# An RWKV layer whose k, r and v products run as plain fp32 on raw weights, with unpadded 64-row products and another order around the inversion

## Chip, cores and metric

The kernel runs on one core of a Trainium2 chip. What is compared is the device time of one execution in microseconds, the median of several. The profiled execution is one more, with a trace of every engine.

## What is computed

The program is a stack of layers on 256 tokens of width 1024: an RWKV time mix, a convolutional feed-forward, two attention layers and several gated feed-forward layers. Only the RWKV time mix is touched by the change:

```python
    xx = jnp.pad(x, ((0, 0), (1, 0), (0, 0)))[:, :-1] - x
    xr, xw, xk, xv, xa, xg = [x + xx * mu[i] for i in range(6)]
    r = xr @ w_rkv[0]
    k = xk @ w_rkv[1]
    v = xv @ w_rkv[2]
    w = -jax.nn.softplus(-(w_decay0 + jnp.tanh(xw @ w_decay1) @ w_decay2)) - 0.5
    a = jax.nn.sigmoid(a0 + (xa @ a1) @ a2)
    g = jax.nn.sigmoid(xg @ g1) @ g2
...
    def step(S, inp):
        r_t, d_t, k_t, v_t, a_t, b_t = inp
        sa = jnp.einsum('bhij,bhj->bhi', S, a_t)
        S = (S * d_t[:, :, None, :] + sa[..., None] * b_t[:, :, None, :]
             + v_t[..., None] * k_t[:, :, None, :])
        return S, jnp.einsum('bhij,bhj->bhi', S, r_t)
```

After the scan come a group norm per head, a bonus term, the gate g and the projection w_o.

## The kernel before

x is kept transposed (feature on the partition) as hT; xx is its difference to the token before. A mix is x + xx*mu for one 128-row chunk: VectorE makes the even chunks (L450), ScalarE and POOL the odd ones (L447, L448).

Weights come in units of 1 MB, on the queue of SyncE, into two raw slots: units 0 to 3 are k, 4 to 7 r, 8 to 11 v, 12 to 15 w_o. Each is split into a rounded part hi (L120, ScalarE, for units 0 and 1 also VectorE) and the rest lo (L122, VectorE; a table of bits in that line gives some quarters to POOL: one of units 0 and 1, all four of units 10 to 13). The activations are split as well (L138, L139), and mm3 (L146 to L148) forms one product from three matmuls of the fast fp32r type:

```python
        W['mm'].append(PE.matmul(o, lhsT=lh, rhs=rh, start=start, stop=False))
        PE.matmul(o, lhsT=lh, rhs=rl, start=False, stop=False)
        PE.matmul(o, lhsT=ll, rhs=rh, start=False, stop=stop)
```

The order is this. The LoRA products pw and pa (L474, L480) need eight mixes each, then pz (L498) in plain fp32 gives decay and a; a scan over time on VectorE (L508) makes the decay sums. k is four units (pk), with a norm per head behind each (pn, pnb); r is four units (pr), with the bonus products pq and pb. AR and KB hold the decayed r and a, and the decayed k and b, head pairs on 128 partitions.

The scan works on four chunks of 64 tokens. For each, M = KB' AR per head is a 64-row product. The kernel copies KB into a tile KZ whose other half is zero (L601) and so uses 128 rows; VectorE masks the result (L606). The diagonal 32x32 blocks of M are transposed into one batch of 32 triangular matrices (L616) and inverted together on VectorE, 31 steps of one product and one sum each (L623, L624), with n(j+1) elements per partition, n = 31 - j:

```python
                    V.tensor_tensor(out=tv, in0=XI[:, j + 1:32, j:j + 1].to_broadcast([P, n, j + 1]), in1=TL[:, j:j + 1, 0:j + 1].to_broadcast([P, n, j + 1]), op=ALU.mult)
                    V.tensor_tensor(out=TL[:, j + 1:32, 0:j + 1], in0=TL[:, j + 1:32, 0:j + 1], in1=tv, op=ALU.add)
```

Two transposes of the result (TtD at L626, TnD at L627) end this chain. Beside it TensorE forms v (pv), transposes KB (pkt), the gate's two products pg (L660, 128 columns) and pg2 (L661, 32 columns), and pgt (L674, L675). Behind the chain pgm and pwm (L693, L709) complete the inverse to 64x64 in Tt, with copies gm; means and centre subtract the head mean from v into vc and UV. Each chunk then takes pak (L745), ry (from chunk 1 on), their sum RHs, pu (L765, the inverse times RHs), psn (the new state) and py (the output). POOL forms the gate terms in five instructions for each half of 128 tokens (`gates`, L809 to L813) and issues broadcast loads of rows (L169); `gn` is the group norm on VectorE.

Each engine's instructions stand in one list; `tc.high_priority()` and `tc.issue_after` shift their place in it. Each engine works its list off in order.

## Time and profile before

| | us |
|---|---|
| median of 3 runs | 1377.85 (1376.36 to 1378.54) |
| profiled execution | 1378.07 |
| its span in the trace | 1376.4 |
| TensorE busy | 1321.2 (96%) |
| VectorE busy | 1071.2 (78%) |
| ScalarE busy | 840.4 (61%) |
| POOL busy | 129.3 (9%) |

The span is from the first to the last instruction of the trace; 1.67 us of the profiled execution lie outside it. A busy time is the sum over all instructions of an engine, so an engine can be far from full over the span and full in one stage. Matmuls are pipelined: the distance between their starts, not their duration, is what one costs.

### The profile page before, as it was taken

How to read it: one execution, taken by the hardware profiler on the slowest of the kernel's cores; microseconds unless marked ns; L12 is line 12 of the kernel's file. 1: busy time of each engine (PE TensorE's matmuls, PEld its weight loads, DVE VectorE, ACT ScalarE, POOL GpSimd, SP SyncE). 2: the span in 40 equal slices, each digit the busy share in tenths (PEclk: the TensorE clock that was granted, in tenths of full speed). 3: DMA queues.
4: the chain of work that ended last, by engine and by line, in shares of the span. 5: the costliest groups of instructions: out<-in, count | busy, mean ns of one | idle time of the engine just before them, and what ended most of it. 6: DMA issues, size and time to landing. Idle time of an engine off the chain costs nothing.

```text
span 1376.4 us, 21002 instructions
## 1 busy us (share of the span) xinstructions
PE 1321.2 (96%) x7776; PEld 1125.3 (82%) x7776; DVE 1071.2 (78%) x2296; ACT 840.4 (61%) x1793; POOL 129.3 (9%) x140
## 2 busy tenths in 40 slices
PE   6789888899999999999999999999999999999998
PEld 4788486688888977888888998888887788888887
DVE  8999968799888776998887986766668787576663
ACT  6675444677667874876667854655545766464551
POOL 3366380000000020000001000000000000000000
PEclk9999888999999999999999999999999999999999
DMA  5343202466553523565536554455553644265550
GB/s 212 125 152 111 74 2 92 154 233 226 185 193 128 184 92 107 199 235 202 202 131 225 200 193 158 172 212 191 199 189 118 254 155 151 78 229 192 197 192 31
DMA packets 35111, 226.30 MB, mean 164 GB/s; under 512 B 3744, under 2 KB 6208, under 8 KB 8896
## 3 DMA queue, kind: packets, MB, share of 16 engines
...
q8 instruction: 61, 1.00, 0.3%
...
## 4 chain that ended last, share of the span: by engine, by line
PE 83%; DVE 12%; ACT 3%; issue 1%; DMA 1%; POOL 1%; DVEq 0%; ACTq 0%; SPq 0%
PE pu L299 9%; PE pm L299 7%; PE pu L297 6%; PE md L148 4%; PE md L146 4%; PE md L147 4%; PE pm L297 4%; PE fd L146 3%; PE fd L147 3%; PE fd L148 3%; DVE lo L122 1%; DVE TL L624 1%; DVE tm L623 1%; PE pu L295 1%; PE gu L148 1%
## 5 line engine op out<-in xcount | busy, mean ns | idle before, releaser
L122 DVE TENSOR_TENSOR lo<-raw,hi 128x512 fp32r<-128x512 f32 x680 | 441.6, 692 | 79.0 <-ACT hi L120 76.9
L120 ACT CAST hi<-raw 128x512 fp32r<-128x512 f32 x696 | 387.5, 618 | 142.8 <-PE md L148 52.3
L299 PE MATMUL pu<-X_n_x,hi 128*128 128x512 f32 x560 | 142.1, 393 | 0.0
L299 PEld LDWEIGHTS pu<-X_n_x,hi 128*128 128x128 f32 x560 | 100.1, 189 | 17.5
L299 PE MATMUL pm<-X_ml_x,hi 128*128 128x512 f32 x392 | 99.7, 393 | 0.0
L297 PEld LDWEIGHTS pu<-X_n_x,lo 128*128 128x128 f32 x640 | 87.4, 190 | 6.2
L297 PE MATMUL pu<-X_n_x,lo 128*128 128x256 f32 x640 | 89.7, 283 | 0.0
L299 PEld LDWEIGHTS pm<-X_ml_x,hi 128*128 128x128 f32 x392 | 70.0, 189 | 12.2
L117 DVE SCALAR_TENSOR_TENSOR lo<-raw,cv,hi 128x256 fp32r<-128x256 f32 (+1 forms) x136 | 67.3, 560 | 14.1 <-ACT hi L116 14.1
L116 ACT ACTIVATE hi<-raw,cv 128x256 fp32r<-128x256 f32 (+1 forms) x136 | 65.9, 560 | 14.5 <-DMA raw<-in_wst 8.9
L305 DVE TENSOR_TENSOR r<-pm,r 128x256 f32<-128x256 f32 x56 | 23.6, 424 | 57.3 <-ACT r L304 57.3
L304 ACT COPY r<-pm 128x256 f32<-128x256 f32 x56 | 20.8, 372 | 74.3 <-PE pm L299 74.3
L297 PEld LDWEIGHTS pm<-X_ml_x,lo 128*128 128x128 f32 x448 | 61.2, 190 | 4.3
L297 PE MATMUL pm<-X_ml_x,lo 128*128 128x256 f32 x448 | 62.7, 282 | 0.0
L939 ACT ACTIVATE ab<-zs,cv 128x256 f32<-128x256 f32 x80 | 47.5, 600 | 16.8 <-DVE zs L305 16.7
L147 PE MATMUL md<-lo,md0h 128*128 128x512 f32 x128 | 49.9, 390 | 0.0
L146 PE MATMUL md<-hi,md0h 128*128 128x512 f32 x128 | 49.8, 389 | 0.0
L148 PE MATMUL md<-hi,md0l 128*128 128x512 f32 x128 | 49.8, 389 | 0.0
L146 PE MATMUL md<-hi,md1h 128*128 128x512 f32 x128 | 49.8, 389 | 0.0
L147 PE MATMUL md<-lo,md1h 128*128 128x512 f32 x128 | 49.8, 389 | 0.0
L148 PE MATMUL md<-hi,md1l 128*128 128x512 f32 x128 | 49.8, 389 | 0.0
L940 DVE SCALAR_TENSOR_TENSOR ab<-zs,cv,ab 128x255 f32<-128x255 f32 x80 | 38.3, 481 | 10.7 <-ACT ab L939 9.2
...
## 6 DMA issues: line engine op xcount, KB each, us to landing
...
```

What stands on the lines that cost most here:

```text
L116: A.activation(hi[:, q:q + w], r[:, q:q + w], AF.Copy, scale=g[:, j:j + 1])
L117: V.scalar_tensor_tensor(out=lo[:, q:q + w], in0=r[:, q:q + w], scalar=g[:, j:j + 1], in1=hi[:, q:q + w].bitcast(F32), op0=ALU.mult, op1=A ...
L120: (A.copy, V.tensor_copy, G.tensor_copy)[(40 if i < W['vhi'] else 0) // (1, 3, 9, 27)[q // SPL] % 3](hi[:, q:q + SPL], r[:, q:q + SPL])
L122: pe_.tensor_tensor(out=lo[:, q:q + SPL], in0=r[:, q:q + SPL], in1=hi[:, q:q + SPL].bitcast(F32), op=ALU.subtract)
L146: W['mm'].append(PE.matmul(o, lhsT=lh, rhs=rh, start=start, stop=False))
L147: PE.matmul(o, lhsT=lh, rhs=rl, start=False, stop=False)
L148: PE.matmul(o, lhsT=ll, rhs=rh, start=False, stop=stop)
L297: W['mm'].append(PE.matmul(pt[:, 0:T], lhsT=l3[:, k, fs], rhs=X2[:, 0, k, :], start=False, stop=False))
L299: PE.matmul(pt, lhsT=h3[:, k, fs], rhs=X2[:, :, k, :], start=False, stop=k == KD - 1)
L305: V.tensor_tensor(out=out, in0=pt[:, 0:T], in1=out, op=ALU.add)
L939: A.activation(ab[:, s, :], z, AF.Identity, bias=cw(3, fi), scale=cw(2, fi))
L940: V.scalar_tensor_tensor(out=ab[:, s, 1:T], in0=z[:, 0:T - 1], scalar=cw(1, fi), in1=ab[:, s, 1:T], op0=ALU.mult, op1=ALU.add)
```

## The change

- The units 0 to 11 stay raw, in six rotating slots (kw), and k, r and v are plain fp32 matmuls on them. All splits of these weights and of their activations go.
- The mixes of the two small LoRA products are folded into their weights (two POOL products on l1); pw has 128 output rows for both, 16 matmuls on hT and xx.
- The mixes for k, r and the gate are formed together before the decay's sigmoids, the one for v during k.
- What follows a k or r unit's norm (k_post, r_post) is issued behind the 13th matmul of the next unit.
- M uses 64 rows of KB and AR without the padding copies; the products of the two halves of the partitions alternate. pak and pu use 64 rows as well, and the memsets of the padding go.
- TnD is transposed before TtD. The block from pgm to pwm has high priority. means and centre work on the first 128 tokens behind the chain, on the others behind the last copy of pwm.
- pgt moves from beside the chain into the scan, behind chunks 0 and 1 of it.
- The splits of the units 12 and 13 move from beside the chain into the scan; their lo goes from POOL to VectorE. A cap keeps splits from being issued before.

```diff
-                    (A.copy, V.tensor_copy, G.tensor_copy)[(40 if i < W['vhi'] else 0) // (1, 3, 9, 27)[q // SPL] % 3](hi[:, q:q + SPL], r[:, q:q + SPL])
-                    pe_ = G if {0: 8, 1: 8, 10: 15, 11: 15, 12: 15, 13: 15, 57: 12, 58: 12, 59: 12}.get(i, 0) >> q // SPL & 1 else V
+                    A.copy(hi[:, q:q + SPL], r[:, q:q + SPL])
+                    pe_ = G if {57: 12, 58: 12, 59: 12}.get(i, 0) >> q // SPL & 1 else V
                     pe_.tensor_tensor(out=lo[:, q:q + SPL], in0=r[:, q:q + SPL], in1=hi[:, q:q + SPL].bitcast(F32), op=ALU.subtract)
...
-        split(i + (len(W['cyc']) if ahead is None else ahead))
+        split(min(i + (len(W['cyc']) if ahead is None else ahead), W['cap']))
...
+            kw = []
+
+            def wload(upto):
+                while len(kw) < upto:
+                    u = len(kw)
+                    tag = ('hi', 'lo')[u % 2] if u % 6 < 4 else 'raw'
+                    kw.append(w0.tile([P, 2048], F32, tag=tag, name=f'kw{u}', bufs=2))
+                    nc.sync.dma_start(kw[u], wst[u])
...
+            for i, w in ((1, 0), (4, 1)):
+                sl = slice(w * 64, w * 64 + 64)
+                j = CV['mu'] + i * 8
+                G.tensor_tensor(out=l1[:, 1, :, sl], in0=l1[:, 0, :, sl], in1=cv[:, j:j + 8].unsqueeze(2).to_broadcast([P, KD, 64]), op=ALU.mult)
...
+            def mixes(i, X):
                 for k in range(KD):
...
-
-            def proj(nm):
-                hi, lo = unit()
-                h3 = hi.rearrange('p (k c) -> p k c', k=KD)
-                l3 = lo.rearrange('p (k c) -> p k c', k=KD)
-                pts = [psum(f'{nm}_{f}') for f in range(2)]
-                for k in range(KD):
-                    for f in range(2):
-                        fs = slice(f * P, f * P + P)
-                        mm3(pts[f][:, 0:T], h3[:, k, fs], l3[:, k, fs], XH[:, k, :], XL[:, k, :], k == 0, k == KD - 1)
-                return [pt[:, 0:T] for pt in pts]
+                    mu = cvc('mu', i * 8 + k)
+                    if k % 2:
+                        A.activation(X[:, k], xx[:, k, :], AF.Copy, scale=mu)
+                        G.tensor_tensor(out=X[:, k], in0=X[:, k], in1=hT[:, k, 1:T + 1], op=ALU.add)
+                    else:
+                        V.scalar_tensor_tensor(out=X[:, k], in0=xx[:, k, :], scalar=mu, in1=hT[:, k, 1:T + 1], op0=ALU.mult, op1=ALU.add)
+            XRK = xp.tile([P, 2, KD, T], F32, tag='XH', name='XRK', bufs=1)
+            XR, XK = (XRK[:, 0], XRK[:, 1])
+
+            def proj(nm, u, X):
+                w3 = kw[u].rearrange('p (k c) -> p k c', k=KD)
+                pts, mms = ([psum(f'{nm}_{f}')[:, 0:T] for f in range(2)], [])
+                for f in range(2):
+                    for k in range(KD):
+                        mms.append(PE.matmul(pts[f], lhsT=w3[:, k, f * P:(f + 1) * P], rhs=X[:, k, :], start=k == 0, stop=k == KD - 1))
+                return (pts, mms)
...
             for k in range(KD):
                 V.tensor_tensor(out=xx[:, k], in0=hT[:, k, 0:T], in1=hT[:, k, 1:T + 1], op=ALU.subtract)
-                PE.matmul(pw[0:64, 0:T], lhsT=l1[:, k, 0:64], rhs=mixk(1, k, (V, G)[k % 2]), start=k == 0, stop=k == KD - 1)
+                PE.matmul(pw[:, 0:T], lhsT=l1[:, 0, k, :], rhs=hT[:, k, 1:T + 1], start=k == 0, stop=False)
+            for k in range(KD):
+                PE.matmul(pw[:, 0:T], lhsT=l1[:, 1, k, :], rhs=xx[:, k, :], start=False, stop=k == KD - 1)
...
-            pa = psum('pa')
-            for k in range(KD):
-                PE.matmul(pa[0:64, 0:T], lhsT=l1[:, k, 64:128], rhs=mixk(4, k, (V, G)[k % 2]), start=k == 0, stop=k == KD - 1)
-            A.copy(gw[0:64, 3, :], pa[0:64, 0:T])
+            A.copy(gw[0:64, 3, :], pw[64:128, 0:T])
...
-            mixsplit(2, 'k')
+            mixes(2, XK)
+            mixes(0, XR)
+            xg = wp.tile([P, KD, T], F32, tag='gt', name='xg')
+            mixes(5, xg)
...
-                pk = proj(f'pk{u}')
+                pk, mms = proj(f'pk{u}', u, XK)
+                if u:
+                    with tc.issue_after(mms[12].ins):
+                        k_post(u - 1, *kn.pop())
...
-                (G if 0 >> u & 1 else V).tensor_tensor(out=blk(KB, u, 1), in0=qb(kkr), in1=eb(Ei, u), op=ALU.mult)
-            mixsplit(0, 'r')
-            xga = W['sa']
+                G.tensor_tensor(out=blk(KB, u, 0), in0=qb(ktu), in1=eb(Ei, u), op=ALU.mult)
+                kn.append((kkr, nb))
+            mixes(3, XK)
...
-                pr = proj(f'pr{u}')
+                pr, mms = proj(f'pr{u}', 4 + u, XR)
+                with tc.issue_after(mms[12].ins):
+                    if u == 0:
+                        k_post(3, *kn.pop())
+                    else:
+                        r_post(pqs)
...
-                            kz = KZ[:, hf]
+                            pms = [psum(f'pm{c}{hf}{e}', 'acc') for e in range(2)]
+                            for jj in range(4):
+                                for e in range(2):
+                                    es_ = slice(e * 64, e * 64 + 64)
+                                    PE.matmul(pms[e][:, jj * P:(jj + 1) * P], lhsT=KB[es_, hf * 4 + jj, csl], rhs=AR[es_, hf * 4 + jj, csl], start=True, stop=True)
                             for e in range(2):
-                                es_ = slice(e * 64, e * 64 + 64)
-                                A.copy(kz[es_, :, e, :], KB[es_, hf * 4:hf * 4 + 4, csl])
-                            for e in range(2):
-                                pm = psum(f'pm{c}{hf}{e}')
-                                for jj in range(4):
-                                    PE.matmul(pm[:, jj * P:(jj + 1) * P], lhsT=kz[:, jj, e, :], rhs=AR[:, hf * 4 + jj, csl], start=True, stop=True)
-                                lastM = V.tensor_tensor(out=M[:, pc, hf * 8 + e * 4:hf * 8 + e * 4 + 4, :], in0=pm.rearrange('p (i x) -> p i x', i=4), in1=mask.unsqueeze(1).to_broadcast([P, 4, P]), op=ALU.mult)
...
+                                V.tensor_tensor(out=M[:, pc, hf * 8 + e * 4:hf * 8 + e * 4 + 4, :], in0=pms[e].rearrange('p (i x) -> p i x', i=4), in1=mask.unsqueeze(1).to_broadcast([P, 4, P]), op=ALU.mult)
...
                 TtD, TnD = (XD, XI)
-                V.transpose(out=TtD.rearrange('p s i -> p i s'), in_=TL)
-                chain = V.transpose(out=TnD.rearrange('p s j -> p j s'), in_=TL.rearrange('p i j -> p j i'))
-            pvs = [modeB_wide(XH, XL, f'pv{hf}') for hf in range(2)]
+                V.transpose(out=TnD.rearrange('p s j -> p j s'), in_=TL.rearrange('p i j -> p j i'))
+                chain = V.transpose(out=TtD.rearrange('p s i -> p i s'), in_=TL)
+            pvs = [[psum(f'pv{hf}_{t}') for t in range(2)] for hf in range(2)]
+            for t in range(2):
+                for hf in range(2):
+                    for k in range(KD):
+                        PE.matmul(pvs[hf][t], lhsT=XK[:, k, t * P:(t + 1) * P], rhs=kw[8 + 2 * hf + k // 4].rearrange('p (k c) -> p k c', k=4)[:, k % 4, :], start=k == 0, stop=k == KD - 1)
+            W.update(dma=12, cv=12, u=12, base=12, cap=12)
+            fetch(12 + RAW_B)
...
-            def centre(gv):
-                with tc.issue_after(gv.ins):
-                    for hf in range(2):
+            def centre(t, after):
+                with tc.issue_after(after.ins):
+                    for hf in range(2 - 2 * t):
                         uv = UV0[hf] = t2k(f'UV0{hf}').rearrange('p (s x) -> p s x', s=8)
                         V.tensor_tensor(out=uv[0:64].rearrange('p (e j) x -> p e j x', e=2), in0=pvs[hf][0][0:64].rearrange('p (j e x) -> p e j x', j=4, e=2), in1=mns[0, hf][0:64].rearrange('p (j e) -> p e j', e=2).unsqueeze(3).to_broadcast([64, 2, 4, 64]), op=ALU.subtract)
-                    for t in range(2):
-                        for hf in range(2):
-                            r = slice(64 if t == 0 and 1 and False else 0, 128)
-                            V.tensor_tensor(out=vc[r, t, hf * 512:(hf + 1) * 512].rearrange('p (h x) -> p h x', h=8), in0=pvs[hf][t][r].rearrange('p (h x) -> p h x', h=8), in1=mns[t, hf][r].unsqueeze(2).to_broadcast([128 - r.start, 8, 64]), op=ALU.subtract)
+                    for hf in range(2):
+                        V.tensor_tensor(out=vc[:, t, hf * 512:(hf + 1) * 512].rearrange('p (h x) -> p h x', h=8), in0=pvs[hf][t].rearrange('p (h x) -> p h x', h=8), in1=mns[t, hf].unsqueeze(2).to_broadcast([P, 8, 64]), op=ALU.subtract)
+            means(0, chain)
+            centre(0, chain)
...
-                    if 0 != at:
+                    if (3, 3, 5, 5)[i] != at:
                         continue
                     t, hf = (i // 2, i % 2)
-                    pgt = psum(f'pgt{t}{hf}', 'acc')
+                    pgt = psum(f'pgt{t}{hf}')
                     sl = slice(hf * 512, hf * 512 + 512)
...
+            with tc.high_priority():
...
+                    for s in range(16):
+                        for s0, s1_, pc in qq:
+                            PE.matmul(pgm[s1_, s * 32:(s + 1) * 32], lhsT=Ms[tp][s0, pc, s, s1_], rhs=TnD[s0, tp * 16 + s, :], start=True, stop=True)
                     for s0, s1_, pc in qq:
-                        PE.matmul(pgm[s1_, s * 32:(s + 1) * 32], lhsT=Ms[tp][s0, pc, s, s1_], rhs=TnD[s0, tp * 16 + s, :], start=True, stop=True)
+                        cpi = (A.copy, V.tensor_copy)[tp](gms[tp][s1_, :], pgm[s1_, :])
+                    ga, gv = (cpi, None) if tp == 0 else (ga, cpi)
...
+                with tc.issue_after(ga.ins), tc.issue_after(gv.ins):
                     for s0, s1_, pc in qq:
-                        PE.matmul(pwm[s0, s * 32:(s + 1) * 32], lhsT=gms[tp][s1_, s * 32:(s + 1) * 32], rhs=TtD[s1_, tp * 16 + s, :], start=True, stop=True)
-                for (s0, s1_, pc), cp in zip(qq, ((A.copy, A.copy), (V.tensor_copy, V.tensor_copy))[tp]):
-                    cp(Tt[s0, tp * 16:tp * 16 + 16, 1, :], pwm[s0, :].rearrange('p (s x) -> p s x', s=16))
...
+                gtgo(1)
+                for tp in range(2):
...
+            means(1, cpl)
+            centre(1, cpl)
...
-                G.memset(UV[as_], 0.0)
...
-                    PE.matmul(pak[as_, s * 64:(s + 1) * 64], lhsT=Ms[t][:, pc, hf * 8 + s, a0:a0 + 64], rhs=UV[:, s, :], start=True, stop=True)
+                    PE.matmul(pak[as_, s * 64:(s + 1) * 64], lhsT=Ms[t][rs_, pc, hf * 8 + s, a0:a0 + 64], rhs=UV[rs_, s, :], start=True, stop=True)
...
-                    PE.matmul(pu[as_, s * 64:(s + 1) * 64], lhsT=Tt[:, t * 16 + hf * 8 + s, :, :].rearrange('p c x -> p (c x)'), rhs=RH[:, s, :], start=True, stop=True)
+                    PE.matmul(pu[as_, s * 64:(s + 1) * 64], lhsT=Tt[as_, t * 16 + hf * 8 + s, :, :].rearrange('p c x -> p (c x)'), rhs=RH[as_, s, :], start=True, stop=True)
...
+                W.update(cap=NU)
+                if c < 2:
+                    with tc.issue_after(ctx_['s'].ins):
+                        split(13 + c)
```

Three places show how the order moves. First TensorE between the gate products and the scan, in the order before (pg and pg2 are the gate's first product, pgt its second, l1g and l2g their weights):

```order
L660 MATMUL pg<-xg,l1g_253 128x256
L661 MATMUL pg_1565<-xg,l1g_253 32x256
L674 MATMUL pgt_1587<-l2g,gg 128x512
L675 MATMUL pgt_1587<-l2g,gg 128x512
L674 MATMUL pgt_1591<-l2g,gg 128x512
L675 MATMUL pgt_1591<-l2g,gg 128x512
L674 MATMUL pgt_1595<-l2g,gg 128x512
L675 MATMUL pgt_1595<-l2g,gg 128x512
L674 MATMUL pgt_1599<-l2g,gg 128x512
L675 MATMUL pgt_1599<-l2g,gg 128x512
L693 MATMUL pgm_1606<-XDL,M_1142 32x32 x32
L693 MATMUL pgm_1641<-XDL,M_1205 32x32 x32
```

Now, from behind the last pkt:

```order
L670 MATMUL pg<-xg,l1g_218 128x256
L671 MATMUL pg_984<-xg,l1g_218 32x256
L704 MATMUL pgm_1009<-XDL,M_685 32x32 x32
L704 MATMUL pgm_1044<-XDL,M_740 32x32 x23
L754 MATMUL pak_1172<-UV_976,M_685 64x64 x8
L704 MATMUL pgm_1044<-XDL,M_740 32x32 x9
L670 MATMUL pg<-xg,l1g_218 128x256
L754 MATMUL pak_1183<-UV_978,M_685 64x64 x8
L671 MATMUL pg_984<-xg,l1g_218 32x256
L670 MATMUL pg<-xg,l1g_218 128x256
```

pgm has moved ahead of the gate pairs, with pak among them. Then the last of these pairs and what follows:

```order
L671 MATMUL pg_984<-xg,l1g_222 32x256
L670 MATMUL pg<-xg,l1g_222 128x256
L671 MATMUL pg_984<-xg,l1g_222 32x256
L719 MATMUL pwm_1085<-XDL,gm_1007 32x32 x32
L719 MATMUL pwm_1120<-XDL,gm_1008 32x32 x32
L774 MATMUL pu_1193<-RHs,Tt 64x64 x8
L684 MATMUL pgt_1241<-l2g,gg 128x512
L774 MATMUL pu_1203<-RHs,Tt 64x64 x8
```

All gate products stood ahead of pgm; now one pair does, and seven stand between pgm and pwm, while pgt stands inside the scan. Second, ScalarE over the same stretch, before (gg is the gate's activation, gt the copy of pgt, gm the copy of pgm):

```order
L662 ACTIVATE gg<-pg 128x256
L663 ACTIVATE gg<-pg_1565 32x256
L344 ACT_TABLE_LOAD
L344 ACTIVATE psq<-gg,epst 1x1
L676 COPY gt<-pgt_1587 128x512
L676 COPY gt<-pgt_1591 128x512
L676 COPY gt<-pgt_1595 128x512
L676 COPY gt<-pgt_1599 128x512
L695 COPY gm_1604<-pgm_1606 32x512 x2
```

and now, with the casts of the units 12 and 13 ahead:

```order
L120 CAST hi_1293<-raw_929 128x512 x4
L120 CAST hi_1421<-raw_931 128x512 x4
L672 ACT_TABLE_LOAD
L672 ACTIVATE gg<-pg 128x256
L706 COPY gm_1007<-pgm_1009 32x512 x2
L712 COPY Tt<-XDL 32x32x32 x2
L721 COPY Tt<-pwm_1085 32x16x32 x2
```

The activation gg reads pg only when its last matmul is done, and the copies of gm stand behind it in both; only now pgm's matmuls are far ahead of pg's last. Third, VectorE in the front end, before (mx_x are splits, EE the decay's sigmoid, ls the scan over time):

```order
L139 TENSOR_TENSOR mx_x<-mix_2_307,mx_x 128x256
L139 TENSOR_TENSOR mx_x<-mix_3_311,mx_x 128x256
L122 TENSOR_TENSOR lo_361<-raw_97,hi_360 128x512
L143 TENSOR_SCALAR EE<-EE 128x512
L139 TENSOR_TENSOR mx_x<-mix_4_316,mx_x 128x256
L450 SCALAR_TENSOR_TENSOR mix_6_325<-HX,cv 128x256
L508 SCALAR_TENSOR_TENSOR ls_336<-cs,EE 128x256
L143 TENSOR_SCALAR EE<-EE 128x512
L139 TENSOR_TENSOR mx_x<-mix_5_320,mx_x 128x256
L508 SCALAR_TENSOR_TENSOR ls_336<-cs,EE 128x256
```

and now, from the difference xx on:

```order
L471 TENSOR_TENSOR HX<-HX 128x256 x8
L456 SCALAR_TENSOR_TENSOR XRK<-HX,cv 128x256 x8
L456 SCALAR_TENSOR_TENSOR xg<-HX,cv 128x256 x4
L143 TENSOR_SCALAR EE<-EE 128x512
L507 SCALAR_TENSOR_TENSOR ls_318<-cs,EE 128x256 x2
L143 TENSOR_SCALAR EE<-EE 128x512
L507 SCALAR_TENSOR_TENSOR ls_323<-cs,EE 128x256 x2
```

The twelve mixes stand in one piece ahead of the first sigmoid; before, mixes, splits and sigmoids alternated.

## Rows read from the trace of the kernel before

**Rows 1.** By stage: stretch, length, busy us (instructions) by engine, granted clock, DMA share, GB/s.
```profile
0.00:31.00 31.00, 19.46 (x82) 12.93 (x83) 25.20 (x60) 19.58 (x48) 11.37 (x19) 1.00 0.63 236
31.00:66.30 35.30, 29.04 (x225) 28.05 (x224) 34.18 (x67) 22.31 (x50) 14.71 (x12) 0.95 0.32 119
66.30:101.10 34.80, 30.53 (x250) 29.54 (x249) 32.63 (x62) 24.20 (x53) 20.99 (x19) 1.00 0.40 142
101.10:118.40 17.30, 16.27 (x137) 15.62 (x136) 15.67 (x31) 14.67 (x26) 6.06 (x7) 1.00 0.05 21
...
163.20:177.00 13.80, 11.23 (x288) 10.60 (x288) 13.06 (x22) 6.13 (x9) 4.51 (x7) 0.50 0.02 4
177.00:186.90 9.90, 9.86 (x144) 9.59 (x144) 3.28 (x6) 5.17 (x11) 9.08 (x9) 0.93 0.01 2
...
196.40:216.90 20.50, 10.50 (x148) 10.21 (x148) 19.69 (x24) 6.68 (x14) 12.84 (x13) 0.75 0.15 52
```
**Rows 2.** VectorE groups, 0 to 118.4 us: count | busy us, mean ns | idle before.
```profile
L122 DVE TENSOR_TENSOR lo<-raw,hi 128x512 fp32r<-128x512 f32 x38 | 29.7, 805 | 0.3 <-ACT hi L120 0.2
L450 DVE SCALAR_TENSOR_TENSOR mix<-HX,cv 128x256 f32<-128x256 f32 x20 | 13.7, 703 | 0.0
L139 DVE TENSOR_TENSOR mx_x<-mix,mx_x 128x256 fp32r<-128x256 f32 x24 | 11.1, 496 | 0.0
L606 DVE TENSOR_TENSOR M<-pm,cs 128x512 f32<-128x512 f32 x16 | 10.5, 684 | 1.1 <-PE pm L605 1.0
```
**Rows 3.** TensorE timeline: start us, length us; pz, then k's and v's split products.
```profile
24.64 6.39 PE L498 MATMUL pz<-gw,l2a 65*128 65x256 f32 x28 [0.78 <-ACT gw L481]
...
31.10 0.28 PE L148 MATMUL pk<-mx_x,lo 128*128 128x256 f32 x1
31.22 0.28 PE L146 MATMUL pk<-mx_x,hi 128*128 128x256 f32 x1
...
119.82 0.39 PE L146 MATMUL pv<-hi,mx_x 128*128 128x512 f32 x1
120.05 0.39 PE L147 MATMUL pv<-lo,mx_x 128*128 128x512 f32 x1
```
**Rows 4.** TensorE timeline: the main piece of the M products.
```profile
102.78 9.20 PE L605 MATMUL pm<-AR,KZ 128*128 128x128 f32 x80 [0.52 <-DVE pq L573]
```
**Rows 5.** VectorE timeline, the chain: its start, two steps, its first closing transpose.
```profile
118.39 2.08 DVE L616 STREAM_TRANSPOSE XDL<-XDL 128x1024 f32<-128x1024 f32 x1 [0.45 <-ACT XDL L611]
...
127.83 1.33 DVE L623 TENSOR_TENSOR tm<-XDL,TL 128x192 f32<-128x192 f32 x1
...
147.37 0.43 DVE L623 TENSOR_TENSOR tm<-XDL,TL 128x256 f32<-128x256 f32 x1
...
159.51 1.91 DVE L626 STREAM_TRANSPOSE XDL<-TL 128x1024 f32<-128x1024 f32 x1
```
**Rows 6.** POOL groups, 118.4 to 165 us, beside the chain.
```profile
L122 POOL TENSOR_TENSOR lo<-raw,hi 128x512 fp32r<-128x512 f32 x16 | 21.9, 1401 | 5.0 <-ACT hi L120 5.0
```
**Rows 7.** TensorE timeline: last gate pair, first pgt, then pgm and pu behind the chain.
```profile
148.77 0.70 PE L660 MATMUL pg<-xg,l1g 128*128 128x256 f32 x2
149.40 0.62 PE L661 MATMUL pg<-xg,l1g 128*32 128x256 f32 x2
149.95 1.13 PE L674 MATMUL pgt<-l2g,gg 128*128 128x512 f32 x2
...
163.30 3.46 PE L693 MATMUL pgm<-XDL,M 32*32 32x32 f32 x122 [4.86 <-DVE XDL L627]
...
177.04 2.69 PE L765 MATMUL pu<-RHs,Tt 128*64 128x64 f32 x32 [0.62 <-ACT RHs L746]
```
**Rows 8.** Timelines of VectorE and POOL in chunk 2 of the scan.
```profile
196.99 9.86 DVE L158 TENSOR_SCALAR rv_gn<-vr,epst 128x8 f32<-128x8 f32 x1
...
207.00 1.72 DVE L158 TENSOR_SCALAR rv_gn<-vr,epst 128x8 f32<-128x8 f32 x1
...
206.78 0.59 POOL L169 DMA_DIRECT2D g_n<-in_rows  x1
```

More of the change, by code (lines that the diff above doesn't have):

```diff
@@ L488, in rwkv @@
             nc.sync.dma_start(l2g, lora2[:, 2:4, :])
+            wload(12)
             av = wp.tile([P, KD, T], F32, tag='av', name='av')
@@ L638, in rwkv, with means @@
             mns = {}
-            with tc.issue_after(chain.ins):
-                for t in range(2):
+            def means(t, after):
+                with tc.issue_after(after.ins):
                     for hf in range(2):
@@ L697, in rwkv @@
[L697 to L711 removed]
+                    G.memset(Tt[s1_, :, 0], 0.0)
@@ new lines, in rwkv @@
+                with tc.issue_after(ga.ins), tc.issue_after(gv.ins):
+                    for s0, s1_, pc in qq:
+                        A.copy(Tt[s0, :, 0], TtD[s0])
+                        V.tensor_copy(Tt[s1_, :, 1], TtD[s1_])
+                gtgo(1)
+                for tp in range(2):
+                    pwm = psum(f'pwm{tp}', 'acc')
+                    for s in range(16):
+                        for s0, s1_, pc in qq:
+                            PE.matmul(pwm[s0, s * 32:(s + 1) * 32], lhsT=gms[tp][s1_, s * 32:(s + 1) * 32], rhs=TtD[s1_, tp * 16 + s, :], start=True, stop=True)
+                    for (s0, s1_, pc), cp in zip(qq, ((A.copy, A.copy), (V.tensor_copy, V.tensor_copy))[tp]):
+                        cpl = cp(Tt[s0, tp * 16:tp * 16 + 16, 1, :], pwm[s0, :].rearrange('p (s x) -> p s x', s=16))
@@ L716, in rwkv @@
             with tc.issue_after(chain.ins):
-                V.memset(SBt, 0.0)
+                G.memset(SBt, 0.0)
             RHs = wp.tile([P, 2, 2, 8, 64], F32, tag='kt', name='RHs')
-            for pc in range(2):
-                V.memset(RHs[(0, 64)[pc]:(64, 128)[pc], pc], 0.0)
             gng, gnb = (grow('gn_g', bns[0:1, 0, 0:1]), grow('gn_b', bns[0:1, 0, 0:1]))
```

93 lines of the change are left out of this document (28 added, 65 removed).

## The prediction

> **What bounds the kernel now.** The change touches only the RWKV layer, which ends near 245 us; behind it both programs run the same code. So I read the span by stages first, then the engine that is full in each, then single instructions. In the stages up to the inversion VectorE is the full engine: 34.18 of 35.3 us during k, 32.63 of 34.8 during r, 15.67 of 17.3 during the decayed products M [rows 1]. Much of that is splitting: 29.7 us of lo and 11.1 us of activation splits, beside 13.7 us of mixes and 10.5 us of M [rows 2]. The inversion that follows (from 118.39 us, L616) is a chain of small VectorE instructions, and TensorE only fills in beside it. Behind the chain TensorE is busy with the scan's products, first at a granted clock of 0.50 (1.2 GHz) [rows 1]. A difference of 0.2%, 2.8 us, is about what a measurement of this kernel can tell from none.
>
> **Term 1, up to the chain.** Removing the lo and the activation splits takes 29.7 + 11.1 = 40.8 us [rows 2] of VectorE's 107.7 us before 118.4 (25.20 in the first 31 us, then the three stages) [rows 1], and four mixes at 0.703 another 2.8. Some 64 us are left: VectorE stops being the bound, and TensorE takes its place. Plain fp32 is dearer there. The 28 records of pz (256 columns, two records per matmul) take 24.64 to 30.68, 0.216 each, 0.431 per matmul; a split product is three matmuls 0.12 apart, 0.36 [rows 3]. A unit of k or r is 16 of these: 6.9 us in place of 5.7. With its four transposes (0.44, at 0.11) and four two-column products (0.8, at some 0.2) a k unit is about 8.1 us, an r unit 7.7; four of each are 63.4 us, against 70.4 before (30.7 to 101.1). I start k at 32, a little later than now, because all twelve k, r and xg mixes of VectorE now stand ahead of the sigmoids (12 x 0.703 = 8.4 us), and ScalarE's twelve stand ahead of the tanh for gw. The single M products between the r units cost 2 to 3 us. r ends at 98.
>
> M before: 80 records in 9.20 us, 0.115 each [rows 4]; all 128 are still there, at 64 rows. Removing ScalarE's KZ copies frees an engine that was not the last to finish, so nothing. If two 64-row products never run at once, the some 105 records left after r take 12 us; VectorE's masks for them (13 x 0.62, from the same back-to-back pace) lie beside it. With the diagonal copies and 0.45 us ahead of the transpose the chain starts at **113** in place of 118.4: **-5.4**. Bounds: 108 if the products overlap, 120 if k starts 5 us later than I say and the switches between 128-row and 64-row products cost 0.1 us each.
>
> **Term 2, the chain.** Before, from L616 to the first product of the result, 118.39 to 163.30, 44.9 us. Clean steps cost what stands from 147.37 to 159.51: 12.1 us for j = 15 to 30, and by symmetry of n(j+1) 11.2 for j = 0 to 14, 23.4 together. Yet a step that takes 0.36 clean (128x192) takes 1.33 at 127.83 [rows 5]. What runs beside it and only there is POOL with 16 lo quarters of 1.40 us, 21.9 us [rows 6]; the steps shrink again when the last is done. The change gives POOL none of them, so the chain is 2.2 + 23.4 + 1.8 (one transpose, since TnD comes first) = 27.4 us: it would end at 140.4. TensorE has to keep up: v is 32 fp32 matmuls of 512 columns, double the 0.431, 27.6 us in place of 96 x 0.228 = 21.9 [rows 3], less two already done, then 24 transposes (2.6) and one pair of gate products (1.2): from 112 to 141.5. So TensorE ends last by a us, and the chain's part is 28.5: **-16.4**. Bounds: -12 (another POOL job meets it), -17.5.
>
> **Term 3, from the chain to the first pu.** Before 13.7 us, 163.30 to 177.04, at half clock behind 4.86 us of idle [rows 7]. Before, gates and pgt fill the time beside the slow chain. Now the order of TensorE holds seven of the eight gate pairs behind pgm, and ScalarE's copy of gm stands behind the gate activation, so it waits for all of them. A pair takes 148.77 to 149.95, 1.18 us [rows 7]: seven are 8.2 us. Worked through: pgm (1 us), wait for UV on VectorE (to about 144.7), pak and pairs to 155.2, gg, two gm copies and two Tt copies (3.1), pwm and its copies (2.5), RHs (1.2): pu at about 162.5, 21 us behind 141.5: **+7.3**. Bounds +3 (UV earlier) and +19 (half clock throughout).
>
> The Trainium skill, "TensorEngine Tiling (Array Packing)", Key Properties, says that a change of tiling mode drains TensorE. It speaks against putting 64-row and 32-row products between full ones. The pairs above, alternately 128 and 32 columns wide, take 1.18 us in place of twice 0.431, so the row agrees. By the bare fp32 price the seven pairs would be 6.0 us, by the row 8.2.
>
> **Term 4, the scan.** Chunk 0 (pu to pu, 9.9 us [rows 1]) gets two of the four pgt pairs, four matmuls of 1.05 [rows 7], 4.2 us between pu and psn; the wait for the UV copies hides about 1: **+3** (0 to 5). Chunk 1: unpadded products alternate with full ones, some twenty switches, and unit 13 is split on VectorE: **+1.5** (0 to 4). Chunk 2: in the present kernel a 0.17 us VectorE instruction at 196.99 takes 9.86 us while POOL runs the gates, and gets through when POOL issues a DMA at 206.78 [rows 8]. That stall stays, since POOL still does the ten gate instructions, and it covers most of the other 4.2 us of pgt: **+1** (-9 to +5). Removed memsets and splits of activations elsewhere lie beside other work: nothing; if their cover went, under 1 us.
>
> **Sum.** -5.4 - 16.4 + 7.3 + 3 + 1.5 + 1 = -9.0 against the profiled execution, 1378.07, which is 0.22 above the median of the three runs: **1369.0**.
>
> **The rivals.** *A, larger gain.* Two 64-row products in different row halves run at once. For it: 122 records of 32x32 pgm in alternate quadrants take 3.46 us at half clock, 0.028 each, while 64-column records of pu at full clock take 0.06 or more [rows 7]; twice the columns at twice the clock should take the same, so two quadrants ran together. Against: the M products share their columns, and no row here shows that form. Price: M bound by VectorE's masks, the chain starts at 108, and v as well: 1364; if the stall of chunk 2 also goes, 1355. The Trainium skill, "TensorE: Matmul & The Clock Gate", states that small-K products in distinct row groups run concurrently; pgm agrees, M would follow. Chance 0.27.
>
> *B, nothing.* The gain before the chain does not come: the front end is held by 5 us by the mixes and weight loads (12 MB in the first stages, six slots), and chunk 2's stall meets ten gate instructions without a DMA between them, +4. 1369 + 5.4 + 4 = 1378. Against: TensorE's k and r need 63 us wherever they start. Chance 0.12.
>
> *C, slower.* Behind the chain TensorE waits for UV and runs short pieces; 4.86 us of idle before pgm was followed by 13.7 us at 0.50 [rows 1, 7]. If the clock falls there, the 14 gate matmuls, pak and pwm (some 12 us) take 12 more and chunk 0 four more: 1369 + 16 = 1385. It decides from 33 us between the chain's end and pu on. For it: waits of 2 to 3 us. Against: TensorE is busy until the chain ends, which it was not before. That the steps of the chain stay at 1.33 for a reason other than POOL would come to the same place, 1385, but their dates fit too well. Chance 0.24.
>
> **How the numbers follow.** Forecast near 1369 (1364.5 to 1375): 0.37; A 0.27, B 0.12, C 0.24. So faster 0.64, same 0.12, slower 0.24. The range reaches down to A with part of the stall, 1356, and up to C without its last us, 1384; about 2 in 10 lie outside.
>
> **What would show it.** Right: no lo on POOL beside the chain; steps at 128x192 near 0.36; L616 starting near 113; transposed TnD 27 to 29 us later; TensorE between k0 and r3 the fuller engine, VectorE below 0.8; the gm copies on ScalarE behind gg; pu about 21 us behind the chain. Wrong: a chain that starts at 118 or later (term 1), steps still above 1 us (term 2), a granted clock of 0.50 between chain and pu (term 3, rival C), M records nearer 0.06 (rival A), or a stall of another length in chunk 2 (term 4).

## The result and the profile after

The changed kernel takes 1384.83 us (median of five runs, 1383.05 to 1387.96) against 1378.45 for the kernel before on the same chip: ratio 1.0053, 95% interval 1.0036 to 1.007. It is slower by half a per cent, where the prediction said 1369.0 and a range up to 1384. The profiled execution took 1383.05 us with a span of 1381.4 us, 5.0 us above the 1376.4 of before.

Where the span changed, by the start of the same instruction in both traces (us; chunks run from one chunk's first pu to the next):

| stretch | before | after | difference |
|---|---|---|---|
| start to the chain (first transpose) | 118.4 | 108.2 | -10.2 |
| chain, to its first closing product | 44.9 | 27.7 | -17.2 |
| chain's end to the first pu | 13.7 | 27.8 | +14.0 |
| chunk 0 | 9.9 | 19.7 | +9.8 |
| chunk 1 | 9.5 | 15.7 | +6.2 |
| chunk 2 | 20.5 | 18.8 | -1.7 |
| chunk 3, to the first wo | 2.0 | 6.5 | +4.4 |
| all behind it | 1157.5 | 1157.0 | -0.5 |

So 27.4 us were won up to the end of the chain, and 34.4 lost in four of the five stretches behind it, the next 90 us: more than all of it. The stage windows show how. First the stretches of the changed kernel that answer to [rows 1] (stretch, length, busy us with instructions for TensorE, its weight loads, VectorE, ScalarE and POOL; granted clock, DMA share, GB/s):

```profile
29.00:60.00 31.00, 31.00 (x163) 27.39 (x163) 16.82 (x47) 15.37 (x35) 9.94 (x9) 1.00 0.34 124
60.00:94.00 34.00, 34.00 (x183) 29.31 (x182) 11.75 (x28) 1.57 (x4) 7.31 (x8) 1.00 0.27 93
94.00:108.20 14.20, 13.99 (x129) 10.05 (x129) 10.47 (x20) 4.93 (x8) 7.25 (x7) 1.00 0.22 75
108.20:135.80 27.60, 27.04 (x83) 13.16 (x81) 25.37 (x65) 3.61 (x8) 1.82 (x1) 1.00 0.22 77
135.80:163.70 27.90, 21.49 (x316) 13.47 (x317) 9.32 (x15) 10.83 (x19) 1.89 (x2) 0.67 0.01 1
163.70:183.40 19.70, 19.70 (x153) 13.73 (x153) 10.72 (x16) 8.59 (x16) 9.61 (x10) 0.69 0.03 5
183.40:199.10 15.70, 15.66 (x150) 12.06 (x149) 6.22 (x11) 5.28 (x9) 8.69 (x9) 0.89 0.16 64
199.10:217.90 18.80, 18.20 (x153) 14.38 (x152) 16.67 (x27) 8.36 (x16) 12.92 (x10) 0.82 0.16 57
```

Up to 94 us TensorE is now the full engine (31.00 of 31, 34.00 of 34) and VectorE about half busy (16.82) or less; with M's masks VectorE is busier (10.47 of 14.2 up to 108), and TensorE stays full. From 135.8 on look at the granted clock: it is at 1.00 until the chain ends, and its mean is 0.67 to 0.89 in every stage behind it. In the chunks 0 and 1 TensorE waits for hardly anything (19.70 busy of 19.70); it is slow at work.

VectorE's groups up to the chain show that no split is left there, and what the mixes and M's masks take now, to be read against [rows 2] (count | busy us, mean ns | idle before):

```profile
L612 DVE TENSOR_TENSOR M<-pm,cs 128x512 f32<-128x512 f32 x16 | 9.9, 683 | 2.4 <-PE pm L610 2.4
L456 DVE SCALAR_TENSOR_TENSOR XRK<-HX,cv 128x256 f32<-128x256 f32 x12 | 9.3, 832 | 0.0
```

The chain on VectorE's timeline (start us, length us), for [rows 5]:

```profile
108.19 1.98 DVE L620 STREAM_TRANSPOSE XDL<-XDL 128x1024 f32<-128x1024 f32 x1 [1.32 <-ACT XDL L615]
...
114.59 0.36 DVE L627 TENSOR_TENSOR tm<-XDL,TL 128x192 f32<-128x192 f32 x1
...
133.68 2.10 DVE L630 STREAM_TRANSPOSE XDL<-TL 128x1024 f32<-128x1024 f32 x1
```

The step of 128x192 that took 1.33 us takes 0.36, and so does its mirror image at 128.60. POOL's groups beside the chain, for [rows 6], are one memset:

```profile
L729 POOL MEMSET vc<- 128x2048 f32 x1 | 1.8, 1818 | 25.3 <-PE pv L636 25.3
```

TensorE's timeline around and behind the chain, for [rows 4] (first line) and [rows 7] (the bracket is idle time before, and who ended it):

```profile
97.72 7.96 PE L610 MATMUL pm<-AR,KB 64*128 64x128 f32 x104
...
135.93 1.93 PE L704 MATMUL pgm<-XDL,M 32*32 32x32 f32 x110 [0.69 <-ACT hi L120]
141.11 1.97 PE L754 MATMUL pak<-UV,M 64*64 64x64 f32 x16 [3.25 <-DVE vc L663]
...
147.71 1.22 PE L670 MATMUL pg<-xg,l1g 128*128 128x256 f32 x2
148.86 1.06 PE L671 MATMUL pg<-xg,l1g 128*32 128x256 f32 x2
...
158.68 0.24 PE L719 MATMUL pwm<-XDL,gm 32*32 32x32 f32 x2 [1.86 <-ACT gm L706]
159.28 3.62 PE L719 MATMUL pwm<-XDL,gm 32*32 32x32 f32 x126 [0.36 <-ACT gm L706]
163.70 1.94 PE L774 MATMUL pu<-RHs,Tt 64*64 64x64 f32 x16 [0.81 <-ACT RHs L755]
165.57 2.07 PE L684 MATMUL pgt<-l2g,gg 128*128 128x512 f32 x2
```

pgm still runs at full clock. Then TensorE waits 3.25 us, since pak stands next in its order and needs UV from VectorE (UV ends at 140.46; the profile names the vc right behind it as what came last), and the granted clock is 0.50 for the next 11 us (mean of 140 to 151): a gate pair takes 2.14 us from start to start. From 152 to 158 the clock is back (0.99). Then TensorE waits again, 1.86 and 0.36 us for gm, pwm runs at half clock, and three of the four pgt matmuls in chunk 0 take 2.07 (0.50 on average from 160 to 175). ScalarE's timeline shows why gm is so late:

```profile
156.34 1.28 ACT L672 ACT_TABLE_LOAD   x1 [16.87 <-PE pg L670]
157.64 0.38 ACT L672 ACTIVATE gg<-pg 128x256 f32<-128x256 f32 x1
158.05 1.18 ACT L706 COPY gm<-pgm 32x512 f32<-32x512 f32 x2
```

ScalarE stands 16.87 us before gg, with the copy of gm behind it, while pgm is long done.

The loss of chunk 1 is of another kind. TensorE's timeline there, changed kernel:

```profile
188.56 0.33 PE L784 MATMUL psn<-UV,KB 128*64 128x64 f32 x2
188.82 0.33 PE L754 MATMUL pak<-UV,M 64*64 64x64 f32 x2
189.08 0.33 PE L784 MATMUL psn<-UV,KB 128*64 128x64 f32 x2
...
193.21 0.47 PE L754 MATMUL pak<-UV,M 64*64 64x64 f32 x2
193.61 0.47 PE L784 MATMUL psn<-UV,KB 128*64 128x64 f32 x2
```

and the same place in the kernel before, both products at 128 rows:

```profile
191.74 0.28 PE L775 MATMUL psn<-UV,KB 128*64 128x64 f32 x2
191.86 0.28 PE L745 MATMUL pak<-UV,M 128*64 128x64 f32 x2
191.98 0.28 PE L775 MATMUL psn<-UV,KB 128*64 128x64 f32 x2
```

From start to start two records took 0.12 us; now, with psn at 128 rows and pak at 64, they take 0.26. From about 193 on they take 0.40, and the clock of 193 to 196 is 0.51, although TensorE was busy for 8.96 of the 9 us from 184 to 193. Chunk 2 repeats it: pak and psn alternate at 0.26 from 207.6 on and at 0.40 from 210.2 on, with a clock of 0.57 from 210 to 217.9.

### The profile page after: what moved, and what is told of

It reads as the page before. It is cut to its first block, busy times and chain, and to the rows that moved or that the text cites. A ratio compares the mean times of both kernels' runs of the same rounds, so it can differ in the third digit from the quotient of the medians.

```text
span 1381.4 us, 20439 instructions
## 1 busy us (share of the span) xinstructions
PE 1346.6 (97%) x7616; PEld 1127.7 (82%) x7616; DVE 1010.3 (73%) x2227; ACT 795.0 (58%) x1701; POOL 93.9 (7%) x104
## 4 chain that ended last, share of the span: by engine, by line
PE 89%; DVE 7%; ACT 2%; issue 1%; DMA 1%; ACTq 0%; DVEq 0%
PE pu L299 9%; PE pm L299 7%; PE pu L297 6%; PE md L148 4%; PE md L147 4%; PE md L146 4%; PE pm L297 4%; PE fd L147 3%; PE fd L148 3%; PE fd L146 3%; PE pr L465 2%; PE pk L465 2%; PE pu L295 1%; PE gu L148 1%; PE gu L147 1%; PE gu L146 1%
## 5 line engine op out<-in xcount | busy, mean ns | idle before, releaser
L122 DVE TENSOR_TENSOR lo<-raw,hi 128x512 fp32r<-128x512 f32 x650 | 419.6, 689 | 78.3 <-ACT hi L120 76.1
L120 ACT CAST hi<-raw 128x512 fp32r<-128x512 f32 x656 | 365.0, 618 | 126.8 <-PE md L148 53.0
L952 ACT ACTIVATE ab<-zs,cv 128x256 f32<-128x256 f32 x80 | 47.4, 600 | 18.4 <-DVE zs L305 18.2
## 6 DMA issues: line engine op xcount, KB each, us to landing
l2g<-in_lora SPq DMA_DIRECT2D x1, 1024.0 KB, 13.8
```

What stands on the lines that cost most here:

```text
L120: A.copy(hi[:, q:q + SPL], r[:, q:q + SPL])
L122: pe_.tensor_tensor(out=lo[:, q:q + SPL], in0=r[:, q:q + SPL], in1=hi[:, q:q + SPL].bitcast(F32), op=ALU.subtract)
L952: A.activation(ab[:, s, :], z, AF.Identity, bias=cw(3, fi), scale=cw(2, fi))
```

## The experiments

Two theories were set against each other first (they aren't the prediction's rivals A and B). A: the loss lies in the order behind the chain (gates between pgm and pwm, gm behind gg, pgt in the scan). B: it lies in the 64-row form of pak and pu.

**B alone: the kernel before, with pak and pu at 64 rows.** UV stays cleared, so the products are the same.

```diff
-lhsT=Ms[t][:, pc, hf * 8 + s, a0:a0 + 64], rhs=UV[:, s, :]
+lhsT=Ms[t][rs_, pc, hf * 8 + s, a0:a0 + 64], rhs=UV[rs_, s, :]
...
-lhsT=Tt[:, t * 16 + hf * 8 + s, :, :]..., rhs=RH[:, s, :]
+lhsT=Tt[as_, t * 16 + hf * 8 + s, :, :]..., rhs=RH[as_, s, :]
```

> The kernel before with one part of the change: pak and pu take 64 rows in place of 128, nothing else. Theory A (the loss comes from the gate products that now stand behind the chain, and the half clock that they meet): the 64-row form is only a bystander, same as before within 2 us. Theory B (the 64-row products cost: each alternation with a full one drains TensorE, and the clock falls beside them): slower by 6 to 10 us, the alternating pak and psn at 0.26 per two records in place of 0.12, and granted clocks under 0.8 in chunks 1 and 2 before POOL's gates start.

Measured: 1384.98 against 1376.98, ratio 1.0057 (1.0039 to 1.0075): two edited lines alone cost what the whole change does. Its windows:

```profile
176.00:186.00 10.00, 9.28 (x101) 8.85 (x101) 2.83 (x6) 3.99 (x8) 3.48 (x4) 0.50 0.01 2
186.00:198.00 12.00, 11.96 (x163) 10.88 (x162) 4.91 (x8) 5.98 (x11) 11.38 (x13) 1.00 0.00 1
198.00:206.00 8.00, 8.00 (x46) 6.72 (x46) 2.60 (x5) 3.22 (x6) 4.84 (x8) 0.61 0.00 0
```

The alternation costs 0.26 per two records here too, and the clock falls with TensorE busy 8.00 of 8.00. Chunk 1 takes 14.9 us in place of 9.5. And chunk 0 takes 14.0 in place of 9.9, for the half clock inherited from behind the chain now lasts through it, up to 186, where before it ended soon after 177 [rows 1]. Part of that is a shift: the first pu now stands among the last records of pak and comes 1.3 us sooner behind the chain, so that from the chain's end to chunk 1 it takes 26.4 us against 23.6. So the edit has two prices in this profile: 2.8 us where the clock is down already, and 5.4 where 64-row products alternate with full ones. In chunk 0 the order changed with the rows (ten records of py stand between the halves of pu, behind a wait of 0.72 us), so this run doesn't show that the rows alone keep the clock down there.

**The same, with pak behind the last psn.**

```diff
+with tc.issue_after(ctx_['psn'].ins) if c else ExitStack():
     PE.matmul(pak[as_, ...
```

> The kernel before with pak and pu at 64 rows, as in before_unpadded (1385.0 us), but pak issued behind the last psn, so that 64-row and 128-row products no longer alternate. Theory S (the alternation costs, directly and by the clock that falls beside it): within 3 us of the kernel before, no granted clock of 0.50 between pu of chunk 1 and chunk 2 before POOL's gates. Theory F (the 64-row form itself costs, fewer rows at work lower the clock): still 5 us or more slower, 0.50 in the same places.

Measured: 1377.45 against 1376.4, ratio 1.0005 (0.9996 to 1.0015). Windows of this kernel:

```profile
176.00:188.00 12.00, 11.28 (x125) 10.78 (x124) 4.62 (x8) 5.75 (x10) 4.90 (x6) 0.54 0.01 1
188.00:206.00 18.00, 17.96 (x279) 17.11 (x277) 11.09 (x17) 9.96 (x18) 17.10 (x21) 1.00 0.01 2
```

Chunk 1 is back at 9.3 us at a clock of 1.00: alternation, not 64 rows, makes that loss. Chunk 0 is still long, 14.1 us. That the total is level has a second reason, in the common code behind; the window from 248 us of this kernel, and of the kernel before:

```profile
248.00:260.00 12.00, 9.77 (x45) 6.52 (x44) 11.79 (x30) 7.64 (x19) 0.53 (x1) 1.00 0.43 146
```
```profile
248.00:260.00 12.00, 8.31 (x33) 5.45 (x33) 9.55 (x25) 5.08 (x12) 0.80 (x2) 0.87 0.78 257
```

Here the clock stays at 1.00 (before 0.87, and 0.84 up to 272), and from the first wo to the end it takes 1152.1 us against 1157.5. So the level time doesn't say that 64 rows are free. In the other kernels' profiles this common stretch takes 1156.2 to 1160.9 us: a total alone, a few us better or worse, doesn't tell what the scan did, and the readings here go by stretches.

**A, its simple form: the gates ahead again.** Without the priority of the block from pgm to pwm (`with tc.high_priority():` becomes `with ExitStack():`), and in a second kernel with pgt ahead of it as well (`at` 0 again).

> The changed kernel without the high priority of the block from pgm to pwm, so all gate pairs stand ahead of pgm again; pgt stays in the scan. Theory A: the first pu comes at 153 to 158 us in place of 163.7, the clock stays up longer, 6 to 12 us faster than the changed kernel, so at or below the kernel before. Theory B: at most 3 us faster, since chunks 0 to 2 keep their length.

> The changed kernel with gate pairs and all pgt ahead of pgm, as in the kernel before. Theory A: pgm starts near 152 us, the first pu at 160 to 164 as now, but chunk 0 takes 10 to 12 us in place of 19.7 and chunk 1 is shorter too: 10 to 14 us faster than the changed kernel. Theory B: 3 to 6 us faster.

Measured: 1385.21, ratio 1.0074 (1.0054 to 1.0093), and 1388.26, ratio 1.0071 (1.0042 to 1.01): no gain, so the simple form of A fell. The profiles say why. pak, which waits for UV, now stood among the gate pairs; the first of the two kernels:

```profile
141.87 1.97 PE L754 MATMUL pak<-UV,M 64*64 64x64 f32 x16 [4.01 <-DVE vc L663]
```

TensorE is idle for 4.01 us before it in both, the clock falls as it did, and pgm, which could have run at once, starts at 154.36 and 169.85. It isn't the place of the gates that counts but what TensorE has to do while UV is missing.

**The changed kernel with pak and pu at 128 rows** (memsets of RHs and UV put back). The order that came out also has two pgt pairs ahead of the first pu.

```diff
-lhsT=Ms[t][rs_, pc, hf * 8 + s, a0:a0 + 64], rhs=UV[rs_, s, :]
+lhsT=Ms[t][:, pc, hf * 8 + s, a0:a0 + 64], rhs=UV[:, s, :]
```

> The changed kernel with pak and pu back at 128 rows, with the memsets of their padding; the scheduler then also puts the two pgt pairs of chunk 0 ahead of pu. Theory A: within 2 us of the changed kernel. Theory B: 6 to 10 us faster than the changed kernel, no granted clock of 0.50 in chunk 1.

Measured: 1373.38 (ten runs), ratio 0.9981 (0.997 to 0.9991): by the ratios 0.7% or 9.9 us below the changed kernel (11.5 between the medians, which come from two chips), at the upper end of what theory B gave or above it. Chunk 1 takes 10.9 us in place of 15.7, and starts 3.4 us sooner, at 179.99; chunk 3 gives 1.8. How much of the 3.4 belongs to the moved pgt pairs wasn't separated. From the chain's end to chunk 1's start it still takes 44 us, at a mean clock of 0.71 and 0.78.

**The same, and gg behind pwm's copies**, so that gm doesn't wait for the gates.

```diff
-A.activation(gg[:, 0, :], pg[:, 0:T], AF.Sigmoid)
...
+with tc.issue_after(cpl.ins):
+    A.activation(gg[:, 0, :], pg[:, 0:T], AF.Sigmoid)
```

> The changed kernel with pak and pu at 128 rows, and the gate's activation issued behind the last copy of pwm, so that the copies of gm no longer wait for the gate products; most gate pairs then stand behind pwm. If what still stands between the chain and pu costs: pu at 150 to 156 us in place of 168.9 in the padded run, 1362 to 1367 us. Rival (the time is given back where the gate terms are needed, in chunk 2's wait of VectorE and POOL): 1370 to 1374, with pu early and chunks 0 to 2 longer.

Measured: 1367.41, ratio 0.9933 (0.992 to 0.9946), 6 us better, though pu comes at 158.4 and not by 156. TensorE's timeline:

```profile
140.91 1.97 PE L758 MATMUL pak<-UV,M 128*64 128x64 f32 x16 [3.19 <-DVE vc L663]
...
146.53 3.62 PE L716 MATMUL pwm<-XDL,gm 32*32 32x32 f32 x128
...
158.44 2.08 PE L778 MATMUL pu<-RHs,Tt 128*64 128x64 f32 x32
```

pwm no longer waits, but the 3.19 us for UV is there, and from 138 to 154 the mean clock is 0.52.

**And four gate pairs ahead of the first pak and of pwm**, so that TensorE has work while it would wait.

```diff
-PE.matmul(pg2[0:32, 0:T], ...)
+W['pg', k] = PE.matmul(pg2[0:32, 0:T], ...)
...
+with tc.issue_after(W['pg', 4].ins):
     PE.matmul(pwm[...
...
+with ExitStack() if c else tc.issue_after(W['pg', 4].ins):
     PE.matmul(pak[...
```

> As gm_first_padded (1367.4 us), but four gate pairs stand ahead of the first pak and of pwm, so that TensorE does not sit idle for 3.2 us while VectorE makes UV. If that idle time is what lets the clock fall to 0.50 from 139 to 155 us: clock 1.00 there, pu at 150 to 153 in place of 158.4, 1360 to 1364 us. Rival (short products keep the clock down whatever stands there): 0.50 as before, within 2 us of 1367.

Measured: 1358.02 (1356.98 to 1358.55) against 1376.39, ratio 0.9866 (0.985 to 0.9883). TensorE's timeline and two windows:

```profile
135.64 2.21 PE L701 MATMUL pgm<-XDL,M 32*32 32x32 f32 x128 [0.70 <-DVE XDL L630]
137.78 0.70 PE L670 MATMUL pg<-xg,l1g 128*128 128x256 f32 x2
...
142.50 2.08 PE L760 MATMUL pak<-UV,M 128*64 128x64 f32 x32
144.50 2.21 PE L717 MATMUL pwm<-XDL,gm 32*32 32x32 f32 x128
...
150.85 2.05 PE L780 MATMUL pu<-RHs,Tt 128*64 128x64 f32 x32 [0.60 <-DVE mn L654]
```
```profile
134.00:151.00 17.00, 15.70 (x323) 9.53 (x322) 14.04 (x22) 12.97 (x22) 3.46 (x5) 1.00 0.10 40
151.00:164.40 13.40, 13.40 (x153) 10.02 (x152) 8.62 (x12) 8.01 (x15) 10.91 (x10) 1.00 0.08 15
```

The wait is filled, the clock stays at 1.00, pwm takes 2.21 in place of 3.62, and the first pu comes 15.2 us after the chain's end in place of 27.8. This beats both kernels, by 18.4 us the one before, and is 2 us better than expected.

**The same order with the change's 64 rows.**

> The changed kernel at its 64 rows for pak and pu, with the order of gates_fill_waits (1358.0 us at 128 rows): gm ahead of the gate's activation, four gate pairs ahead of pak and pwm. What it is slower than 1358.0 is the price of the 64-row form once nothing else lowers the clock. Theory S: 4 to 9 us, 1362 to 1367, with 0.50 or records at 0.13 where pak and psn alternate. Rival (the price came from the half clock that was there already): under 2 us. If the order is the larger part of the loss, it stays well below the kernel before.

Measured: 1363.6 against 1375.36, ratio 0.9907 (0.9891 to 0.9923). Windows:

```profile
134.00:175.00 41.00, 40.11 (x603) 29.47 (x601) 27.65 (x45) 26.61 (x45) 20.37 (x19) 1.00 0.18 64
175.00:183.00 8.00, 8.00 (x37) 5.81 (x37) 2.81 (x5) 1.21 (x2) 1.57 (x2) 0.57 0.01 2
```

The clock is 1.00 up to 175, and falls where pak and psn alternate in chunk 1, TensorE busy 8.00 of 8.00. By the ratios the order is worth 1.5% (1.0053 to 0.9907, some 20 us), and at the good order the 64-row form costs 0.4%, 5.6 us. Sum: the change with its order mended and its rows full is 0.9866.

**64 rows with pak behind psn**, in the changed kernel and in one that also has gg behind pwm (the two edits shown above).

> The changed kernel, pak and pu still at 64 rows, with pak issued behind the last psn, so that they no longer alternate. Theory S (the alternation is what padding took away): 1372 to 1377 us, near the padded run. Rival (behind the chain the 64-row form loses by itself, since pu also alternates with pgt there): 1379 us or more.

> The changed kernel at 64 rows with pak behind psn, as in after_apart, and the gate's activation behind pwm as in gm_first_padded. Theory S: 1366 to 1371 us, as gm_first_padded with its 128 rows. Rival (64 rows lose by themselves): 1373 us or more.

Measured: 1383.04, ratio 1.0046 (1.0031 to 1.0061), and 1373.59, ratio 0.9978 (0.9966 to 0.9991). In the first, chunk 1 falls to 11.2 us, 4.5 less, but chunk 0 takes 22.3, and TensorE then waits 7.16 us before chunk 3's pu and runs at 0.50 up to 226: the gain was given back. The second, with the order half mended, runs at half clock from 140 to 164, where the same edit with full rows (the kernel of 1367.41 us) has its clock back near 155; here pu stands among the gate pairs at half clock. Both times are on the side of the rivals that were written down: issuing pak behind psn mends chunk 1, but not the whole loss of the 64-row form. What holds the clock down longer behind the chain, the rows or the order that comes with them, was not separated.

**POOL beside the chain.** The changed kernel, with one copy and 16 useless subtractions of 128x512 on POOL's own scratch tile beside the chain.

```diff
+with tc.issue_after(x0.ins):
+    G.tensor_copy(dum[:, 1024:2048], XI.rearrange('p s t -> p (s t)'))
+    for i in range(16):
+        q = i % 2 * 512
+        G.tensor_tensor(out=dum[:, q:q + 512], in0=dum[:, 1024:1536], in1=dum[:, 1536:2048], op=ALU.subtract)
```

> The changed kernel with a POOL copy and 16 POOL subtractions of 128x512 on a scratch tile beside the chain, which serve nothing. If POOL held the steps in the kernel before: steps beside them take 1.2 to 1.4 us, the chain 41 to 45 us in place of 27.6, the end 8 to 16 us later. Rival (the splits' other traffic held the steps): the chain stays below 31 us.

Measured in one execution: 1400.99 us. POOL's piece, and a step beside it and its mirror image behind it:

```profile
110.52 20.59 POOL L626 TENSOR_TENSOR dum<-dum 128x512 f32<-128x512 f32 x16
```
```profile
125.98 1.30 DVE L633 TENSOR_TENSOR tm<-XDL,TL 128x192 f32<-128x192 f32 x1
...
143.78 0.36 DVE L633 TENSOR_TENSOR tm<-XDL,TL 128x192 f32<-128x192 f32 x1
```

With POOL at work the chain takes 43.7 us to its first closing product (44.9 in the kernel before, 27.7 in the changed one): POOL is what held the steps. A step of 0.36 takes as long as one of POOL's subtractions (20.59 / 16 = 1.29). The Trainium skill, "SBUF — State Buffer", in "SBUF: two separate sides", says that a VectorE operation with two SBUF inputs and a POOL operation that reads SBUF lock each other out for a whole instruction; these rows agree.

**M's products, four of one half in a row** in place of the halves in turn.

```diff
-for jj in range(4):
-    for e in range(2):
+for e in range(2):
+    for jj in range(4):
```

> The changed kernel with the M products of one row half after the other, four in a row, where they alternate between the halves. If alternating halves ran together: M records at 0.105 to 0.11 in place of 0.077, the chain starts 2 to 4 us later. Rival (the records are just shorter with 64 rows): no difference over 1 us.

Measured in one execution: 1386.52 us. TensorE's timeline:

```profile
98.26 7.88 PE L610 MATMUL pm<-AR,KB 64*128 64x128 f32 x104
```

That is 0.076 per record, against 0.0765 in turn: no difference. So the rate isn't due to the alternation of the halves, and why 64-row records of M take less than the 0.115 of 128 rows [rows 4] stays open.

## Why the prediction was wrong

**Term 1 held, on the good side.** -10.2 measured, -5.4 forecast. TensorE did become the bound. k started at 28.8 in place of 32, since pz ended sooner (32 records at 21.55, 7.42 us long), though a mix took 0.83 in place of the 0.703 of [rows 2]; k and r took 64.7 us, 1.3 less than allowed. M's records are a third shorter, but pb and four v records (94.77 and 96.69) stood between, so that r's end to chain's start took 14.7 us where 15 were allowed. The start at 108 is the number of rival A, yet not by its mechanism: it is mostly the earlier k.

**Term 2 held.** -17.2 against -16.4. The steps are clean, the cause is shown by putting POOL work back, and TensorE's work beside it (60 records of v in 26.02 us, the transposes, one gate pair) ends at 135.2, with the chain and not a us behind it.

**Term 3 failed, at the clock.** The prediction took the gate pairs at 1.18 and pwm at 2.5 with its copies, 21 us in all. The waits were as foreseen: UV late, gm behind gg; idle on TensorE adds up to only 6.4 us between 135.8 and 163.7. But the clock fell to 0.50 in the first of them, 3.25 us, and again at the second, 1.86 us; pak and three pairs, and then pwm, took about twice the time: 27.8 us. Both ends of the term's bounds (+3, +19) held it, +14.0; the value taken from between was wrong. Its argument, that a TensorE busy until the chain's end would stand a wait of 2 to 3 us, doesn't hold here.

**Term 4 failed by most.** Chunk 0: +9.8, where +3 with 5 as the bound was given. The two pgt pairs stood there as said, but three of their four matmuls took 2.0 from start to start and not the 1.05 of [rows 7], and pu and psn around them at half clock too. Chunk 1: +6.2, with 4 as the bound. With full rows it takes 10.9, so 4.8 us belong to the 64-row form; the other 1.4 remain with full rows too, and one of the pgt pairs stands here and not in chunk 2. The twenty switches were named, and priced at 1.5 us together. They came in that number (19 from 188.56 to 194.01), but cost 0.14 each (0.26 against 0.12), 2.7 us; and what no term held, the clock fell behind them, so that the pgt matmul at 194.01 takes 2.08 in place of 1.13. Chunk 2: -1.7, within its bounds; the 9.86 us of [rows 8] are gone (1.56 us for two at 205.49), though POOL runs its ten gate instructions there as before, from 204.98 to 218.2: beside them alone the stall doesn't come, and why it went stays open. Chunk 2 still takes 18.8, since TensorE now has work in it (18.20 us busy, before 10.50 [rows 1]): a pgt pair, and the alternation with the half clock behind it. Luck, then, that the term came near. Chunk 3, +4.4, wasn't in the sum: where the first wo stood right behind pu, four records of pyt and half of py now stand before it: 2.0 us became 6.5, at a mean clock of 0.74 with a 1.11 us wait.

The misses add up: -4.8 and -0.8 on the good side, +6.7 in term 3, +6.8, +4.7, -2.7 and +4.4 in the scan, -0.5 behind it: 13.8 of the 14.0 between -9.0 and +5.0.

**The rivals.** C had the right place, the right mechanism for the order's part and the time, 1385. Its price lay elsewhere, though: 33 us behind the chain and four in chunk 0, where 27.8 us and 9.8 in chunk 0 were measured; and the second mechanism, 64-row products alternating with full ones, was not in it. That its sum is the measured time is luck: up to the chain's end the kernel did 5.6 us better than forecast, from there to pu some 5 us better than C gave, and the scan lost 9 us more. With 0.24 it was rated too low: the one row that spoke to it, half clock behind 4.86 us of idle [rows 7], was set aside for an argument that no row bore out. The Trainium skill's rule that was cited in the prediction ("TensorEngine Tiling (Array Packing)", Key Properties: a change of tiling mode drains TensorE) agrees with the psn and pak rows, which give 0.14 us for each switch. A: M's rate doesn't depend on the turns of the halves, so no run here shows two of them together. B fell: the front end gained.

What stays open: how the 9.9 us of full rows in the changed kernel divide between alternation, the longer half clock and the moved pgt, and why M's records are shorter.
